# Key stacks by DMA, query projections by token halves, ordered VectorE norm chains and later low weight parts in a two-layer fp32 block

## The chip, the cores and the metric

The kernel runs on one core of a Trainium2 chip. The metric is the device time of one execution in microseconds (us). The engines are called as the profile calls them: PE (TensorE), PEld (its weight loads), DVE (VectorE), ACT (ScalarE), POOL (GpSimd) and SP (the engine that issues the DMAs).

## The reference

Two transformer layers on 512 latent tokens and 256 context tokens, width 1024, in fp32. Layer 0 mixes with gated linear recurrences, layer 1 with windowed attention (16 query heads of 64, 4 key heads, context keys, a sink). Each layer is followed by a gated feed-forward part, and each branch goes through a root-mean-square norm and a residual sum. Only the latent tokens are returned.

```python
for l in range(DEPTH):                       # DEPTH = 2
    u_lat = modulate(x_lat, ng[0], ml[0], ml[1])
    u_ctx = modulate(x_ctx, ng[0], mc[0], mc[1])
    if l % 2 == 0:
        y_lat, y_ctx = recurrent_mixer(...)
    else:
        y_lat, y_ctx = attention_mixer(...)  # q, k, v = u @ w_qkv, rope, softmax, @ w_o
    x_lat = x_lat + ml[2] * rms_norm(y_lat, ng[1])
    h_lat = swiglu(modulate(x_lat, ng[2], ml[3], ml[4]), ffn_w_in[l], ffn_w_out[l])
    x_lat = x_lat + ml[5] * rms_norm(h_lat, ng[3])
    ...                                      # the same for the context, in layer 0
```

## The kernel before

Activations lie transposed: 128 partitions hold 128 of the 1024 channels, the free axis holds tokens, and eight such tiles make a stream. For fp32 accuracy each product is made of three: weights and activations are split into a high part (`hi`, rounded) and a low part (`lo`, the rest), and PE adds hi·hi, hi·lo and lo·hi. `wload` fetches a weight tile of 128x1024 by a DMA on SP (`raw`, 4 buffers), makes `whi` on ACT or POOL and `wlo` on DVE or POOL (3 buffers each). Which engine does which is set for each phase by `engines(ph)`: a list for the high parts (a = ACT, p = POOL) and one for the low parts (d = DVE, p = POOL), taken in turn. `whold` does the same and keeps the parts (`kwh`, `kwl`). One accumulation over 1024 channels is 24 matmuls.

Work is written as Python generators, one step per yield. `drain` runs one to its end, and `merge(main, side, ratio)` puts `ratio` steps of `side` behind each step of `main`. The framework then schedules by a timeline of its own, so the order on each engine is a planner's, except where `follow(key, ins)` chains an instruction behind the last one of the same key and engine.

Two passages between stages matter here. At the first, layer 0's feed-forward output `po` ends in two token halves `HS[0]`, `HS[1]`; `lat_next(h)` then does the residual sum and the next norm of half h (`residual`: `y` times the norm factor, added into `xl`; `Acc.add`: squares on ACT, summed on POOL or DVE into `acc`; `rstd_bc`: a sum over partitions on PE, root, reciprocal, broadcast on PE into `ps_tr`; `norm_mod`: `nt`, `uh` on ACT, `ul` on DVE). The K and V projections of context and latent halves (`kv_ctx`, `kv_lat`) run beside `lat_next(1)`. Then come the first four Q projections (`q_lat(range(4))`, 512 tokens wide) and the attention scores, and the other four Q projections beside these. `k_stack` writes each 64-row key head twice, into both halves of the partitions, high and low parts apart (`KC`, `KL`): four ACT copies and four DVE subtractions for each pair of heads.

At the second passage the attention output projection `wo(1)` runs beside `lat_next2(0)`, and layer 1's first feed-forward tiles (`ffn_in`, phase `f1`) beside `lat_next2(1)`.

Of the kernel before, what the change touches and what calls it, by code (L numbers as in the profile page):

```python
# [11 lines left out]
F32 = mybir.dt.float32  # L12
# [7 lines left out]
P = 128  # L20
# [25 lines left out]
def block_kernel(ctx, tc, plan, xT, cT, vecs, w2, cst, atm, rope, ada, rec_a, rec_v, rec_g, rec_o, qk_w, v_w, wo_w, ff_in, ff_out, out):  # L46
# [8 lines left out]
    def uid(s):  # L55
        state["n"] += 1
        return f"{s}{state['n']}"
# [56 lines left out]
        return tiles[k // st.r][:, k % st.r, :]  # L114


    cfg = {"hi": "p", "lo": "d", "n": 0, "pri": 0, "evp": 150, "ll": False}

    def wload(src, n):
        with ExitStack() as es:  # L120
            if cfg["pri"]:
                es.enter_context(tc.high_priority(offset=cfg["pri"]))
            raw = wp.tile([P, 1024], F32, name=uid("raw"), tag="raw", bufs=WB + 1)
            nc.sync.dma_start(out=raw[:, :n], in_=src)
            hi = wp.tile([P, 1024], F32R, name=uid("whi"), tag="whi", bufs=WB)
            lo = wp.tile([P, 1024], F32R, name=uid("wlo"), tag="wlo", bufs=WB)
            q = cfg["n"]
            cfg["n"] += 1
            if cfg["hi"][q % len(cfg["hi"])] == "p":
                nc.gpsimd.tensor_scalar(hi[:, :n], raw[:, :n], 1.0, 0.0, ALU.mult, ALU.add)  # L130
            else:
                nc.scalar.copy(hi[:, :n], raw[:, :n])  # L132
            (nc.gpsimd if cfg["lo"][q % len(cfg["lo"])] == "p" else nc.vector).tensor_sub(  # L133
                lo[:, :n], raw[:, :n], hi[:, :n].bitcast(F32))
        return hi, lo

    def whold(src, n=1024):
# [245 lines left out]
            a.add(t, full(st))  # L383
        return a

    def norm_mod(tiles, acc, G, sh, j, u, sl, st=None):
# [6 lines left out]
        key = uid("nm") if 1 else None  # L393

        def low(i, t):
            if acc is None and 0:
# [28 lines left out]
            low(*v_)  # L425
        yield

    def residual(tiles, ys, yacc, gg, j, xacc, sl, pat=""):

        st = yacc.st  # L430
        bc = rstd_bc(yacc, sl)
        key = uid("res") if 1 else None
        yield
        for i in range(st.ntile):
            y = ys[i][:, :, sl]
            p_ = pat and pat[i] == "p"
# [12 lines left out]
            if xacc is not None:
                xacc.add(tiles[i][:, :, sl], sl, None, i >= st.ntile - 0)  # L450
            yield

    def new_u(st, alloc=None):
# [79 lines left out]
    def engines(ph):  # L533
        cfg["pri"] = {}.get(ph, 200)
        cfg["ll"] = ph in []
        cfg["hi"], cfg["lo"] = {'co': ['a', 'ddp'], 'rb': ['p', 'ddp'], 'ci': ['a', 'd'], 'kv': ['a', 'ddp'], 'wo': ['pa', 'd'], 'l0': ['a', 'd'], 'f1': ['a', 'd'], 'lo2': ['p', 'dp'], 'kw': ['a', 'd']}.get(ph, ("p", "d"))

    def drain(*gens):
        for g in gens:
# [747 lines left out]
    u3 = new_u(SL)  # L1287

    def lat_next(h):
        yield from residual(xl, yl2, yla2, gg2, 0, xla, HS[h], {'ln1': 'pppppppp', 'lw1': 'dpdpdpdp', 'lw0': 'pdddpddd', 'la0': 'dpdpdpdd', 'la1': 'dpdpdpdd', 'ln0': 'dddpdddp', 'cm': 'pdddpddd', 'lm': 'dddpdddp'}.get("ln%d" % h, ""))  # L1290
# [61 lines left out]
    def kv_ctx():  # L1352
        for m in range(2):
            p_ = qk_proj(8 + m, uc3, SC, FC)
            kc = ut([P, 256], name="kc")
            nc.scalar.copy(kc, p_)
            k_stack(kc, m, 0, 256)
            yield
        yield from v_proj(SC, uc3, range(2), 0)

# [6 lines left out]

    QS = {}

    def q_lat(ms):  # L1370
        for m in ms:
            y = roped(qk_proj(m, u3, SL, FL), FL)
            for h in range(2):
                q = ut([P, 512], F32R, name="QS")
# [4 lines left out]
                QS[2 * m + h] = q  # L1379
# [357 lines left out]
```

## Time and profile before

| | |
|---|---|
| three runs, median (lowest to highest) | 1818.57 us (1816.07 to 1819.11) |
| the profiled execution, its own time | 1819.26 us |
| span of its profile | 1817.5 us |
| PE busy in the span | 1744.9 us, 96% |
| DVE, ACT, POOL busy | 1058.1, 741.9, 437.6 us |

The span is what the profiler saw between the first and the last instruction; the execution's own time is 1.8 us longer. PE's busy time counts a matmul from its start to its modelled end, so a matmul at half clock, or one with a gap shorter than its own tail, also reads as busy.

### The profile page before, as it was taken

The page shows a single profiled execution, that of the slowest core. Times are in us where ns is not written, and L with a number is a line of the kernel's source. Part 1 is how long each engine was busy: PE and PEld are TensorE (multiplying, and loading weights), DVE is VectorE, ACT ScalarE, POOL GpSimd, SP SyncE. Part 2 cuts the span into 40 slices and gives each one's busy share as a digit, 9 for nine tenths or more (in the row PEclk, how much of TensorE's full clock was granted, in tenths as well). Part 3 has the DMA queues.
Part 4 walks back from the last instruction along what each step waited for, and adds up shares of the span by engine and source line. Part 5 has one row for each costly group of instructions (what it writes and reads, how often), then busy time and mean ns, then how long its engine had stood idle before and what let it go on. Part 6 is the DMA issues. An engine that isn't in the chain of part 4 may idle for free. (4 is left out here: it accounts for less than half of the span.)

```text
span 1817.5 us, 27788 instructions
## 1 busy us (share of the span) xinstructions
PE 1744.9 (96%) x10991; PEld 1482.3 (82%) x10991; DVE 1058.1 (58%) x1717; ACT 741.9 (41%) x1309; POOL 437.6 (24%) x460
## 2 busy tenths in 40 slices
PE   6899999999899999999999999899899899999997
PEld 3887778788798999988888888787677898888886
DVE  4986444664856744898642535679855853322336
ACT  3653445342654644542222222444665652222211
POOL 3655412433411004500000002424444400000015
PEclk8989999999999999999999999889999999999999
DMA  9435557212143554576554423402011343233323
GB/s 337 127 96 176 173 170 250 88 50 68 47 140 117 168 175 134 164 270 220 166 180 135 152 73 101 130 25 71 12 48 47 116 126 97 90 94 109 101 65 113
DMA packets 83699, 228.15 MB, mean 126 GB/s; under 512 B 9297, under 2 KB 14161, under 8 KB 83569
## 3 DMA queue, kind: packets, MB, share of 16 engines
q1 hardware_dynamic: 83568, 226.38, 38.6%
q8 instruction: 86, 1.41, 0.3%
q14 instruction: 45, 0.36, 0.1%
HBM read 224.25 MB, written 2.10 MB: 125 GB/s over the span
## 5 line engine op out<-in xcount | busy, mean ns | idle before, releaser
L133 DVE TENSOR_TENSOR wlo<-raw,whi 128x1024 fp32r<-128x1024 f32 (+3 forms) x296 | 358.7, 1213 | 315.0 <-ACT whi L132 234.2
L132 ACT CAST whi<-raw 128x1024 fp32r<-128x1024 f32 (+2 forms) x199 | 201.1, 1012 | 466.7 <-issue 177.7
L130 POOL TENSOR_SCALAR whi<-raw 128x1024 fp32r<-128x1024 f32 (+1 forms) x113 | 126.2, 1119 | 774.2 <-PE ps_mm L180 354.4
L180 PE MATMUL ps_mm<-uh,whi 128*128 128x256 f32 (+1 forms) x840 | 290.9, 347 | 2.1 <-POOL whi L130 1.9
L180 PE MATMUL ps_mm<-uh,wlo 128*128 128x256 f32 (+1 forms) x840 | 287.1, 342 | 5.1 <-DVE wlo L133 5.1
L180 PE MATMUL ps_mm<-ul,whi 128*128 128x512 f32 (+1 forms) x840 | 287.4, 342 | 0.0
L180 PE MATMUL ps_kv<-uh,whi 128*128 128x512 f32 (+1 forms) x696 | 247.1, 355 | 0.0
L180 PE MATMUL ps_kv<-uh,wlo 128*128 128x512 f32 (+1 forms) x696 | 245.1, 352 | 1.6 <-DVE wlo L133 1.5
L180 PE MATMUL ps_kv<-ul,whi 128*128 128x512 f32 (+1 forms) x696 | 245.3, 352 | 0.0
L180 PEld LDWEIGHTS ps_mm<-uh,whi 128*128 128x128 f32 x840 | 161.6, 193 | 24.9 <-POOL whi L130 3.3
L180 PEld LDWEIGHTS ps_mm<-uh,wlo 128*128 128x128 f32 x840 | 161.4, 192 | 23.2 <-DVE wlo L133 5.8
L180 PEld LDWEIGHTS ps_mm<-ul,whi 128*128 128x128 f32 x840 | 161.6, 192 | 17.0 <-issue 0.5
L346 POOL TENSOR_TENSOR acc<-acc,sq 128x256 f32<-128x256 f32 (+1 forms) x79 | 91.5, 1160 | 257.1 <-ACT sq L345 256.4
L180 PEld LDWEIGHTS ps_kv<-uh,whi 128*128 128x128 f32 x696 | 132.1, 190 | 22.4 <-issue 2.5
L180 PEld LDWEIGHTS ps_kv<-uh,wlo 128*128 128x128 f32 x696 | 131.7, 189 | 19.5 <-DVE wlo L133 1.9
L180 PEld LDWEIGHTS ps_kv<-ul,whi 128*128 128x128 f32 x696 | 131.9, 190 | 17.3 <-issue 0.3
L191 PE MATMUL ps_mm<-wlo,uh 128*128 128x256 f32 x344 | 100.1, 292 | 8.7 <-DVE wlo L133 8.7
L190 PE MATMUL ps_mm<-whi,uh 128*128 128x256 f32 x344 | 102.1, 299 | 0.8 <-ACT gate L786 0.5
L283 DVE SCALAR_TENSOR_TENSOR aacc<-ar,s,aacc 128x512 f32<-128x512 f32 x112 | 81.7, 756 | 35.1 <-DMA ar<-in_ada_dram 34.3
L180 PE MATMUL ps_kv<-hh,whi 128*128 128x512 f32 (+1 forms) x282 | 100.2, 355 | 0.0
L180 PE MATMUL ps_kv<-hh,wlo 128*128 128x512 f32 (+1 forms) x282 | 100.0, 355 | 0.0
L180 PE MATMUL ps_kv<-hl,whi 128*128 128x512 f32 (+1 forms) x282 | 99.9, 354 | 0.0
(322 smaller groups left out, 3534.3 us busy)
## 6 DMA issues: line engine op xcount, KB each, us to landing
raw<-in_ff_in_dram SPq DMA_DIRECT2D x138, 512.0 KB, 3.6
ar<-in_ada_dram SPq DMA_DIRECT2D x192, 256.0 KB, 4.2
raw<-in_ff_out_dram SPq DMA_DIRECT2D x52, 512.0 KB, 3.5
raw<-in_rec_a_dram SPq DMA_DIRECT2D x34, 512.0 KB, 4.2
raw<-in_rec_v_dram SPq DMA_DIRECT2D x16, 512.0 KB, 3.6
raw<-in_rec_g_dram SPq DMA_DIRECT2D x16, 512.0 KB, 3.5
raw<-in_rec_o_dram SPq DMA_DIRECT2D x16, 512.0 KB, 4.3
raw<-in_wo_w_dram SPq DMA_DIRECT2D x14, 512.0 KB, 3.5
```

The lines of the kernel that those rows point to most:

```text
L130: nc.gpsimd.tensor_scalar(hi[:, :n], raw[:, :n], 1.0, 0.0, ALU.mult, ALU.add)
L132: nc.scalar.copy(hi[:, :n], raw[:, :n])
L133: (nc.gpsimd if cfg["lo"][q % len(cfg["lo"])] == "p" else nc.vector).tensor_sub(lo[:, :n], raw[:, :n], hi[:, :n].bitcast(F32))
L180: mm(ps_, a, b, start=(i == 0), stop=(i == len(q) - 1))
L190: mm(ps, ah, hi[:, s], start=(k == 0), stop=False)
L191: mm(ps, ah, lo[:, s], start=False, stop=False)
L283: nc.vector.scalar_tensor_tensor(a, raw, s_, a, ALU.mult, ALU.add)
L346: (nc.vector if i else nc.gpsimd).tensor_add(d, d, q)
```

## The change

1. `k_stack` makes the high and the low part of a pair of key heads once, 128 partitions wide (one ACT cast, one DVE subtraction), and writes both into both halves of `KC` and `KL` by eight DMAs on SP (64 partitions of 1 KB each). There are six such calls.
2. `q_lat` takes a token slice. The first four Q projections are done for `HS[0]` right behind `kv_lat(0)`, inside the merge with `lat_next(1)`, and for `HS[1]` behind `kv_lat(1)`. Their weights are loaded and split twice.
3. In phase `kv` all low weight parts are made on POOL (before: two of three on DVE).
4. `residual` and `norm_mod` take a key. Both halves of `lat_next` share the key `next`, so that on each engine these steps stand in the order of the program. `lat_next2` has one key for each half.
5. `lat_next(1)` adds six of its eight residual tiles on DVE instead of none; the squares of the last two tiles of `lat_next` and `lat_next2`, and of the last output tile of a half-width feed-forward end, are no longer summed on POOL or DVE but read by PE directly (`own`).
6. `behind`: in phase `f1` the low weight parts of `wload` stand behind the last DVE step of `lat_next2(0)`.

```diff
+    def behind(ins):
+        k = (cfg["behind"], str(ins.ins.engine))
+        if k in lane:
+            tc.add_manual_dep(ins.ins, lane[k], mybir.DependencyInfo(mybir.DependencyClass.NoSync,
+                                                                     mybir.DependencyReason.DATA), reason="behind")
...
-            (nc.gpsimd if cfg["lo"][q % len(cfg["lo"])] == "p" else nc.vector).tensor_sub(
-                lo[:, :n], raw[:, :n], hi[:, :n].bitcast(F32))
+            behind((nc.gpsimd if cfg["lo"][q % len(cfg["lo"])] == "p" else nc.vector).tensor_sub(
+                lo[:, :n], raw[:, :n], hi[:, :n].bitcast(F32)))
...
-                xacc.add(tiles[i][:, :, sl], sl, None, i >= st.ntile - 0)
+                xacc.add(tiles[i][:, :, sl], sl, None, i >= st.ntile - own)
...
-                    yacc.add(y, sl, 0, m >= KD - 0)
+                    yacc.add(y, sl, 0, n == 256 and m >= KD - 1)
...
     def lat_next(h):
-        yield from residual(xl, yl2, yla2, gg2, 0, xla, HS[h], {...}.get("ln%d" % h, ""))
-        yield from norm_mod(xl, xla, G1, ada1[0], 0, u3, HS[h])
+        yield from residual(xl, yl2, yla2, gg2, 0, xla, HS[h], "dddpdddp", "next", 2)
+        yield from norm_mod(xl, xla, G1, ada1[0], 0, u3, HS[h], key="next")
...
     def k_stack(src, m, c0, n):
-        for h in range(2):
-            kv = 2 * m + h
-            a = src[64 * h : 64 * h + 64, :n]
-            own, oth = slice(64 * h, 64 * h + 64), slice(64 - 64 * h, 128 - 64 * h)
-            kh, kl = kcols(0, kv, c0, n), kcols(1, kv, c0, n)
-            nc.scalar.copy(kh[own], a)
-            nc.scalar.copy(kh[oth], a)
-            nc.vector.tensor_sub(kl[own], a, kh[own].bitcast(F32))
-            nc.vector.tensor_sub(kl[oth], a, kh[own].bitcast(F32))
+        th, tl = ut([P, 512], F32R, name="kth")[:, :n], ut([P, 512], F32R, name="ktl")[:, :n]
+        nc.scalar.copy(th, src)
+        nc.vector.tensor_sub(tl, src, th.bitcast(F32))
+        for i, t in enumerate((th, tl)):
+            for h in range(2):
+                for o in range(2):
+                    nc.sync.dma_start(out=kcols(i, 2 * m + h, c0, n)[64 * o : 64 * o + 64].bitcast(F32),
+                                      in_=t[64 * h : 64 * h + 64].bitcast(F32))
...
     engines("kv")
-    drain(merge(seq(kv_ctx(), kv_lat(0)) if 1 else seq(kv_lat(0), kv_ctx()), lat_next(1), 2.5))
-    drain(kv_lat(1))
-    drain(q_lat(range(4)))
+    QH = range(4)
+    drain(merge(seq(kv_ctx(), kv_lat(0), q_lat(QH, HS[0])), lat_next(1), 2.5))
+    drain(kv_lat(1), q_lat(QH, HS[1]))
...
     engines("f1")
+    cfg["behind"] = "next2a"
```

Three places show how instructions move. In the rows, a name is the tile written, then those read; the last part is the shape.

The first is DVE at the first passage, inside the norm of latent half 0 (`nt`, `ul` with `ps_tr_11068` before, `ps_tr_11070` after). Before:

```order
L440 SCALAR_TENSOR_TENSOR y_8072<-y_8072,gv_3263,ps_tr_11164 128x256
L440 SCALAR_TENSOR_TENSOR y_8073<-y_8073,gv_3263,ps_tr_11164 128x256
L440 SCALAR_TENSOR_TENSOR y_8074<-y_8074,gv_3263,ps_tr_11164 128x256
L1326 TENSOR_TENSOR KC_11109<-kc_11147,KC_11107 64x256
L1327 TENSOR_TENSOR KC_11109<-kc_11147,KC_11107 64x256
L440 SCALAR_TENSOR_TENSOR y_8075<-y_8075,gv_3263,ps_tr_11164 128x256
L440 SCALAR_TENSOR_TENSOR y_8076<-y_8076,gv_3263,ps_tr_11164 128x256
L1326 TENSOR_TENSOR KC_11109<-kc_11147,KC_11107 64x256
L1327 TENSOR_TENSOR KC_11109<-kc_11147,KC_11107 64x256
L440 SCALAR_TENSOR_TENSOR y_8077<-y_8077,gv_3263,ps_tr_11164 128x256
L440 SCALAR_TENSOR_TENSOR y_8078<-y_8078,gv_3263,ps_tr_11164 128x256
L401 SCALAR_TENSOR_TENSOR ul_10929<-nt_11078,ada_8211,uh_10921 128x256
```

After:

```order
L408 SCALAR_TENSOR_TENSOR ul_10928<-nt_11080,ada_8211,uh_10920 128x256
L417 SCALAR_TENSOR_TENSOR nt_11088<-xl_7298,gv_10465,ps_tr_11070 128x256
L408 SCALAR_TENSOR_TENSOR ul_10929<-nt_11084,ada_8211,uh_10921 128x256
L417 SCALAR_TENSOR_TENSOR nt_11092<-xl_7300,gv_10465,ps_tr_11070 128x256
L408 SCALAR_TENSOR_TENSOR ul_10930<-nt_11088,ada_8211,uh_10922 128x256
L417 SCALAR_TENSOR_TENSOR nt_11096<-xl_7302,gv_10465,ps_tr_11070 128x256
L408 SCALAR_TENSOR_TENSOR ul_10931<-nt_11092,ada_8211,uh_10923 128x256
L417 SCALAR_TENSOR_TENSOR nt_11100<-xl_7304,gv_10465,ps_tr_11070 128x256
L408 SCALAR_TENSOR_TENSOR ul_10932<-nt_11096,ada_8211,uh_10924 128x256
L408 SCALAR_TENSOR_TENSOR ul_10933<-nt_11100,ada_8211,uh_10925 128x256
L451 TENSOR_TENSOR y_8071<-y_8071,ps_tr_11170 128x256
L454 SCALAR_TENSOR_TENSOR xl_7290<-y_8071,gv_3263,xl_7290 128x256
```

Before, the eight residual products of half 1 (L440) and the key subtractions (L1326, L1327) stand between the second and the third `ul` of half 0; after, all eight `ul` of half 0 stand ahead of the first residual step of half 1.

The second is PE behind the V projection of half 0 (`ps_kv_11433` before, `ps_kv_11451` after). Before:

```order
L191 MATMUL ps_kv_11433<-kwl_10916,uh_10926 128x256
L192 MATMUL ps_kv_11433<-kwh_10915,ul_10934 128x256
L369 MATMUL ps_tr_11299<-ident,rs_11297 128x128 x2
L180 MATMUL ps_kv_11464<-uh_10919,kwh_10837 128x256
L180 MATMUL ps_kv_11503<-uh_10919,kwh_10891 128x256
L190 MATMUL ps_mm_11542<-kwh_10901,uh_10919 128x256
```

After:

```order
L198 MATMUL ps_kv_11451<-kwl_10915,uh_10925 128x256
L199 MATMUL ps_kv_11451<-kwh_10914,ul_10933 128x256
L187 MATMUL ps_kv_11488<-uh_10918,whi_11484 128x256
L187 MATMUL ps_kv_11488<-ul_10926,whi_11484 128x256
L187 MATMUL ps_kv_11488<-uh_10918,wlo_11485 128x256
L187 MATMUL ps_kv_11488<-uh_10919,whi_11484 128x256
```

Before, the broadcast of half 1's norm factor (L369) and matmuls that need half 1's `uh` follow at once; after, four Q projections of half 0 (96 matmuls) stand between, with the sums of half 1's squares among them.

The third is ACT at the second passage, around the first `uh` of `lat_next2(0)` (`uh_13949` before, `uh_14137` after). Before:

```order
L132 CAST whi_14375<-raw_14373 128x1024
L459 COPY y_12722<-ps_mm_14066 128x256
L345 ACTIVATE sq_14098<-ps_mm_14066 128x256
L132 CAST whi_14426<-raw_14424 128x1024
L154 CAST kwh_14325<-raw_14323 128x512
L154 CAST kwh_14329<-raw_14323 128x512
L417 ACTIVATE uh_13949<-nt_14012,ada_9162 128x256
L417 ACTIVATE uh_13950<-nt_14015,ada_9162 128x256
```

After:

```order
L139 CAST whi_14566<-raw_14564 128x1024
L139 CAST whi_14620<-raw_14618 128x1024
L466 COPY y_12912<-ps_mm_14258 128x256
L352 ACTIVATE sq_14290<-ps_mm_14258 128x256
L424 ACTIVATE uh_14137<-nt_14204,ada_9162 128x256
L424 ACTIVATE uh_14138<-nt_14207,ada_9162 128x256
L161 CAST kwh_14472<-raw_14470 128x512
L161 CAST kwh_14476<-raw_14470 128x512
```

Two casts of kept parts have moved behind the first two `uh`; the two high parts of `f1` (`whi`) still stand ahead of them. On DVE the first low part of `f1` stood right ahead of the first `nt` before, and stands behind the last `ul` of that half after.

## Rows read from the trace of the kernel before

**Rows 1.** The page's first part: busy time, share of the span, instructions.

```profile
PE 1744.9 (96%) x10991; PEld 1482.3 (82%) x10991; DVE 1058.1 (58%) x1717; ACT 741.9 (41%) x1309; POOL 437.6 (24%) x460
```

**Rows 2.** Busy time by windows: length, PE, PEld, DVE, ACT, POOL, PEclk, DMA, GB/s.

```profile
1150.30:1218.60 68.30, 55.96 (x372) 53.50 (x371) 48.37 (x110) 29.89 (x73) 22.22 (x27) 0.83 0.16 49
1218.60:1234.70 16.10, 16.10 (x73) 13.33 (x72) 14.43 (x18) 3.30 (x5) 6.00 (x5) 1.00 0.21 67
1234.70:1320.00 85.30, 79.43 (x503) 59.52 (x502) 72.61 (x217) 50.74 (x119) 38.05 (x43) 1.00 0.12 38
...
1160.00:1167.00 7.00, 7.00 (x60) 7.00 (x60) 6.86 (x14) 2.40 (x6) 4.42 (x5) 1.00 0.47 145
```

**Rows 3.** PE's timeline at the first passage: start, length, tile, [idle before, releaser].

```profile
1153.12 0.80 PE L362 MATMUL ps_tr<-ones,acc 128*128 128x1 f32 x4 [2.57 <-POOL acc L346]
...
1176.23 0.42 PE L180 MATMUL ps_mm<-uh,kwh 128*128 128x256 f32 x1
...
1181.87 0.58 PE L180 MATMUL ps_kv<-ul,kwh 128*128 128x256 f32 x1 [5.22 <-DVE ul L401]
...
1198.59 0.80 PE L180 MATMUL ps_kv<-uh,kwh 128*128 128x256 f32 x2 [2.83 <-ACT uh L417]
...
1234.67 0.28 PE L1424 MATMUL ps_kv<-KC,QS 128*128 128x256 f32 x1
```

**Rows 4.** ACT's timeline there.

```profile
1151.37 0.42 ACT L345 ACTIVATE sq<-y 128x256 f32<-128x256 f32 x1 [1.33 <-DVE y L518]
```

**Rows 5.** DVE's timeline there.

```profile
1157.64 1.22 DVE L133 TENSOR_TENSOR wlo<-raw,whi 128x1024 fp32r<-128x1024 f32 x1
1158.78 0.41 DVE L444 TENSOR_TENSOR y<-y,ps_tr 128x256 f32<-128x256 f32 x1
1159.23 2.17 DVE L447 SCALAR_TENSOR_TENSOR xl<-y,gv,xl 128x256 f32<-128x256 f32 x1
...
1171.94 0.87 DVE L410 SCALAR_TENSOR_TENSOR nt<-xl,gv,ps_tr 128x256 f32<-128x256 f32 x2 [0.94 <-PE ps_tr L369]
```

**Rows 6.** POOL's timeline there.

```profile
1158.63 2.50 POOL L133 TENSOR_TENSOR wlo<-raw,whi 128x1024 fp32r<-128x1024 f32 x1 [4.88 <-ACT whi L132]
...
1175.20 4.73 POOL L442 TENSOR_TENSOR xl<-xl,y 128x256 f32<-128x256 f32 x6 [5.86 <-DVE y L440]
```

**Rows 7.** DVE's groups, forms apart, 1150 to 1235 us: count | busy, mean ns | idle before.

```profile
L401 DVE SCALAR_TENSOR_TENSOR ul<-nt,ada,uh 128x256 fp32r<-128x256 f32 x16 | 8.3, 516 | 0.8 <-ACT uh L417 0.7
...
L410 DVE SCALAR_TENSOR_TENSOR nt<-xl,gv,ps_tr 128x256 f32<-128x256 f32 x16 | 7.4, 474 | 1.0 <-PE ps_tr L369 0.9
...
L440 DVE SCALAR_TENSOR_TENSOR y<-y,gv,ps_tr 128x256 f32<-128x256 f32 x10 | 4.3, 475 | 0.0
...
L1326 DVE TENSOR_TENSOR KL<-ry,KL 64x256 fp32r<-64x256 f32 x8 | 3.4, 420 | 0.6 <-ACT KL L1324 0.2
...
L1327 DVE TENSOR_TENSOR KC<-kc,KC 64x256 fp32r<-64x256 f32 x4 | 2.5, 635 | 0.1
...
L444 DVE TENSOR_TENSOR y<-y,ps_tr 128x256 f32<-128x256 f32 x6 | 2.5, 410 | 0.0
```

**Rows 8.** The view of the tile `raw`, 1140 to 1235 us: its DMAs.

```profile
L124 SPq DMA_DIRECT2D raw<-in_qk_w_dram x8: 327/328/383, 1142.8 to 1221.9; - x8
DMA to landing us min/median/max: 3.5/3.6/4.4
```

**Rows 9.** The second passage, timelines of ACT, DVE and PE.

```profile
1430.07 1.05 ACT L132 CAST whi<-raw 128x1024 fp32r<-128x1024 f32 x1 [6.00 <-DMA raw<-in_ff_in_dram]
...
1431.15 1.22 DVE L133 TENSOR_TENSOR wlo<-raw,whi 128x1024 fp32r<-128x1024 f32 x1 [4.17 <-ACT whi L132]
...
1434.19 0.58 PE L180 MATMUL ps_mm<-uh,kwh 128*128 128x256 f32 x1 [3.52 <-ACT uh L417]
```

**Rows 10.** The end, timelines of POOL and DVE.

```profile
1805.35 0.72 POOL L346 TENSOR_TENSOR acc<-acc,sq 128x256 f32<-128x256 f32 x1 [0.67 <-ACT sq L345]
...
1806.72 0.50 DVE L447 SCALAR_TENSOR_TENSOR xl<-y,gv,xl 128x256 f32<-128x256 f32 x1
```

More of the change, by code (lines that the diff above doesn't have):

```diff
@@ L114, in ch @@
         return tiles[k // st.r][:, k % st.r, :]
-    cfg = {"hi": "p", "lo": "d", "n": 0, "pri": 0, "evp": 150, "ll": False}
+    cfg = {"hi": "p", "lo": "d", "n": 0, "pri": 0, "evp": 150, "ll": False, "behind": None}
+    def behind(ins):
[3 more added lines that the diff above has]
+                                                                     mybir.DependencyReason.DATA), reason="behind")
     def wload(src, n):
@@ L384, in sumsq, with norm_mod @@
         return a
-    def norm_mod(tiles, acc, G, sh, j, u, sl, st=None):
+    def norm_mod(tiles, acc, G, sh, j, u, sl, st=None, key=None):
         if acc is not None:
@@ L392, in norm_mod @@
         late = []
-        key = uid("nm") if 1 else None
+        key = key or uid("nm")
         def low(i, t):
@@ L426, in norm_mod, with residual @@
         yield
-    def residual(tiles, ys, yacc, gg, j, xacc, sl, pat=""):
+    def residual(tiles, ys, yacc, gg, j, xacc, sl, pat="", key=None, own=0):
         st = yacc.st
         bc = rstd_bc(yacc, sl)
-        key = uid("res") if 1 else None
+        key = key or uid("res")
         yield
@@ L535, in engines @@
         cfg["ll"] = ph in []
-        cfg["hi"], cfg["lo"] = {'co': ['a', 'ddp'], 'rb': ['p', 'ddp'], 'ci': ['a', 'd'], 'kv': ['a', 'ddp'], 'wo': ['pa', 'd'], 'l0': ['a', 'd'], 'f1': ['a', 'd'], 'lo2': ['p', 'dp'], 'kw': ['a', 'd']}.get(ph, ("p", "d"))
+        cfg["hi"], cfg["lo"] = {'co': ['a', 'ddp'], 'rb': ['p', 'ddp'], 'ci': ['a', 'd'], 'kv': ['a', 'p'], 'wo': ['pa', 'd'], 'l0': ['a', 'd'], 'f1': ['a', 'd'], 'lo2': ['p', 'dp'], 'kw': ['a', 'd']}.get(ph, ("p", "d"))
     def drain(*gens):
@@ L1289, in lat_next @@
     def lat_next(h):
-        yield from residual(xl, yl2, yla2, gg2, 0, xla, HS[h], {'ln1': 'pppppppp', 'lw1': 'dpdpdpdp', 'lw0': 'pdddpddd', 'la0': 'dpdpdpdd', 'la1': 'dpdpdpdd', 'ln0': 'dddpdddp', 'cm': 'pdddpddd', 'lm': 'dddpdddp'}.get("ln%d" % h, ""))
-        yield from norm_mod(xl, xla, G1, ada1[0], 0, u3, HS[h])
+        yield from residual(xl, yl2, yla2, gg2, 0, xla, HS[h], "dddpdddp", "next", 2)
+        yield from norm_mod(xl, xla, G1, ada1[0], 0, u3, HS[h], key="next")
     if "kv" == "po0":
@@ L1354, in kv_ctx @@
             p_ = qk_proj(8 + m, uc3, SC, FC)
-            kc = ut([P, 256], name="kc")
-            nc.scalar.copy(kc, p_)
-            k_stack(kc, m, 0, 256)
+            k_stack(p_, m, 0, 256)
             yield
@@ L1368, in block_kernel, with q_lat @@
     QS = {}
-    def q_lat(ms):
+    def q_lat(ms, sl=FL):
         for m in ms:
-            y = roped(qk_proj(m, u3, SL, FL), FL)
+            y = roped(qk_proj(m, u3, SL, sl), sl)
             for h in range(2):
-                q = ut([P, 512], F32R, name="QS")
+                if 2 * m + h not in QS:
+                    QS[2 * m + h] = ut([P, 512], F32R, name="QS")
+                q = QS[2 * m + h][:, sl]
                 a = y[64 * h : 64 * h + 64]
@@ L1378, in q_lat @@
                 nc.vector.scalar_tensor_tensor(q[oth], a, 0.125, q[own].bitcast(F32), ALU.mult, ALU.subtract)
-                QS[2 * m + h] = q
             yield
     engines("kv")
-    drain(merge(seq(kv_ctx(), kv_lat(0)) if 1 else seq(kv_lat(0), kv_ctx()), lat_next(1), 2.5))
-    adat[0] = "o"
-    if "kv" == "kv":
-        drain(ada_gen(1, tuple([]), ada1))
-    drain(kv_lat(1))
+    QH = range(4)
+    drain(merge(seq(kv_ctx(), kv_lat(0), q_lat(QH, HS[0])), lat_next(1), 2.5))
+    drain(kv_lat(1), q_lat(QH, HS[1]))
     H2.close()
@@ L1512, in lat_next2 @@
     def lat_next2(h):
-        yield from residual(xl, yw, ywa, gg1, 0, xla1, HS[h], {'ln1': 'pppppppp', 'lw1': 'dpdpdpdp', 'lw0': 'pdddpddd', 'la0': 'dpdpdpdd', 'la1': 'dpdpdpdd', 'ln0': 'dddpdddp', 'cm': 'pdddpddd', 'lm': 'dddpdddp'}.get("lw%d" % h, ""))
+        key = "next2" + "ab"[h]
+        yield from residual(xl, yw, ywa, gg1, 0, xla1, HS[h], ("pdddpddd", "dpdpdpdp")[h], key, 2)
         if not u4:
             u4.extend(new_u(SL))
-        yield from norm_mod(xl, xla1, G2, ada1[3], 0, u4, HS[h])
+        yield from norm_mod(xl, xla1, G2, ada1[3], 0, u4, HS[h], key=key)
     drain(merge(piped([(b, kv) for kv in range(4) for b in (2, 3)], AD), wo(0), 0.09))
@@ L1536, in block_kernel @@
                     ffn_in(SL, 1, u4, hl1, range(N0), HS[1], 0, hold_f, kf)), lat_next2(1), 2.2))
+    cfg["behind"] = None
     yf, yfa = new_ys(SL), Acc(SL, DY)
```

## The prediction

> **What bounds the kernel now.** I read the page's first part, then windows of the three places that the diff touches, then each engine's timeline there. PE is busy for 96% of the span [rows 1], so a gain must come from stretches in which PE waits or runs at half clock, or from fewer or cheaper matmuls. The change removes no product of the reference, so I looked for the lost time.
>
> The first passage reaches from 1150.3 us, where PE runs out of feed-forward work, to the first score at 1234.67 [rows 2, 3]: 84.4 us. The program has 312 matmuls of 256 columns and 96 of 512 in it. At full clock the first kind starts every 0.12 us (60 in 7.00 us) and the second every 0.22 us (73 in 16.10) [rows 2]: 37.4 and 21.6 us, 59 in sum. So some 25 us are lost. About 12.3 of them are open gaps (68.30 less 55.96 busy [rows 2]), mainly three. One is 2.57 us until POOL has summed the last squares. One is 5.22 us until DVE makes an `ul` of half 0. One is 2.83 us until ACT makes a `uh` of half 1 [rows 3]. The rest is half clock: the granted clock has a mean of 0.83 there and 1.00 in the windows behind [rows 2], and a single matmul's row reads 0.42 and 0.58 us there against 0.28 at full clock [rows 3].
>
> Why DVE is late is in its order and not in its load (48.4 of 68.3 us busy [rows 2]): eight residual products and four key subtractions stand between the `ul` tiles for which PE waits. POOL then needs 4.73 us for six of half 1's residual sums, and had waited 5.86 for DVE [rows 6].
>
> Elsewhere there is less to win. Scores take 79.4 us of PE in 85.3, with DVE at 72.6 [rows 2]. At the second passage PE waits 3.52 us for a `uh` [rows 9]. The end is a chain of POOL and DVE [rows 10].
>
> **The first passage, term by term.** I walk the chain in the new order, with durations from the rows.
>
> *Own squares.* Before, the last square ends on ACT at 1151.79 [rows 4] and PE reads the sum at 1153.12 [rows 3]. After, PE reads the square itself: it starts at about 1152.0, 1.1 us earlier. With the 24 matmuls that fill the broadcast (2.9 us) PE is at 1155.7 or so by then.
>
> *Residual of half 0.* It began at 1158.78, with a 1.22 us low part ahead of it on DVE [rows 5] that now is POOL's. I put the start at 1156.1. From there to the first `nt` it took 13.16 us (to 1171.94 [rows 5]). After, one POOL sum of 0.7 us less stands at its end (by the one at the end of the kernel [rows 10]), and more POOL low parts run beside it (below): I take 13.7, so `nt` at 1169.8. PE has 96 context matmuls (11.5 us) until 1167.3 and waits until the first `uh` at 1170.6: a gap of 3.3 us stays, in a new place.
>
> *Norm of half 0.* Its 16 steps now stand together. At 0.47 to 0.52 each by the means [rows 7], nearer 0.42 where nothing blocks, with two key low parts, they end at 1178. PE follows with 72 matmuls to about 1179.2. The 5.22 us gap is gone.
>
> *Residual of half 1.* On DVE behind that, with two rope sets (2 us) ahead of or between its tiles: 13.7 + 2, so `nt` at about 1194. Six tiles' sums are DVE's now, 6 x 0.50 [rows 10] against POOL's 4.73 [rows 6]. PE has one V and three Q accumulations of half 0 (96 matmuls, 11.5 us) until 1190.7, then waits for squares and a late POOL low part, and ends the fourth Q at about 1195. Here a wait of 2 to 3 us takes the place of the old 2.83.
>
> *Norm of half 1, then Q.* 16 norm steps and some 21 of rope and query rows at 0.43 (16 us), plus 5 us of blocking: 1215. PE runs 120 of its 192 matmuls within that and 72 behind (8.6 us): first score at 1223.6 against 1234.67. **Term 1: -11.2 us.** Splitting Q costs PE 192 x 0.12 against 96 x 0.22, about +1.5 us, and is in the walk. Bounds: if every new wait doubles, -5; if the gaps close and the clock stays at full, 60.5 us of matmuls (504 x 0.12) and some 6 of unavoidable chain remain, -18.
>
> **What blocks DVE.** A residual step with two operands from memory (L447) took 2.17 us at 1159.23 and ended at 1161.40, just behind a POOL low part that ran from 1158.63 to 1161.13 [rows 5, 6]. Alone it takes 0.50 [rows 10]. Steps with a PSUM operand (L444) keep 0.41 [rows 5, 7]. Context key subtractions take 635 ns where POOL sums beside them, against 420 for the same form on the latent keys [rows 7]. The change makes all eight low parts of Q on POOL, 2.50 us each [rows 6]: 20 us in which DVE could stand still. I take half of that, 10 us in all, of which some 7 are on the chain: DVE steps that read PSUM or that stand before PE's need go on, and the low parts whose weights come early lie under context work. Both ends: 0 and 16.
>
> The Trainium skill, page "SBUF — State Buffer", section "Who interferes with whom", has a rule that speaks against this change: a DVE instruction with two SBUF inputs contends with a GpSimd instruction that reads SBUF, and whichever issues first keeps the shared pair for its whole length. The row of 2.17 us agrees. By the rule alone each of the eight low parts would block a residual or norm step, and the gain would be the first rival's.
>
> **The key stacks.** DVE loses 24 subtractions at 0.42 to 0.64 [rows 7], about 11.5 us, and gains six of 128x256 (2.5) and the residual sums (3). The low parts that go to POOL free another 2.4 (2 x 1.22 [rows 5]); query rows in halves cost 1 to 2, blocking 10. DVE's load over both windows and the scores stays near 137 us: moved, not lowered. Less of it is left when the scores begin, where DVE is at 85%: **Term 2: -1.0 us** (0 to -3).
>
> The copies go to SP: 48 of 64 KB. No such transfer is in the trace; the nearest row is a 512 KB weight, 0.33 us to issue and 3.5 to 4.4 us to land [rows 8]. In the new order each copy waits for the one eight places earlier, so 48 go in six groups: 2.6 us each if issue alone counts (8 x 0.33), 4.4 if landing does. The first 32 stand behind the low parts of half 0's keys (about 1190) and end by 1198. Queued behind them is the fourth Q weight of half 1, needed near 1215: no cost. The last 16 follow at about 1217 and land by 1224 to 1226; the first score that reads these keys is near 1231. I cost them at nothing, hidden by the first scores; from 14 us for both groups on, each us would be paid.
>
> **The other terms.** *Second passage:* DVE's first `nt` there comes up to 4.17 us earlier, since no low part that waits for its weight stands ahead [rows 9]. But ACT still has two high parts ahead of the first `uh`, and the weight for them lands at 1430.07 [rows 9]; `uh` moves only by what is queued behind them. **Term 3: -2.5** (-1 to -5, between the low part's 1.22 and all that the low part holds up). *End:* 0.72 us of POOL goes [rows 10], but DVE's last residual step ends at 1807.2 and the factor behind the sum is needed after it. **Term 4: -0.4** (0 to -0.7). *Other stages:* the planner places instructions of layer 0's recurrences otherwise, without a change in the code. **Term 5: 0** (-3 to +3).
>
> Sum: -11.2 - 1.0 - 2.5 - 0.4 = -15.1, against this execution's 1819.26: 1804.2. It lies 0.7 above the median of 1818.57, so I predict 1803.5.
>
> **Rivals.**
> - *POOL's low parts block DVE fully (0.16).* For it: the 2.17 us row [rows 5]. Against: only steps that meet a low part wait. 16 us on the chain instead of 7 are 9 more, of which the Q matmuls that fill PE's waits cover 3: 6 us lost of term 1, 1809.5.
> - *DVE is the bound, so the order gains nothing (0.14).* For it: 72.6 of 85.3 us in the scores [rows 2], and a load that stays the same; what PE wins until the first score it gives back waiting for softmax steps. Term 1 shrinks to the 1.1 of the squares, with 0.4 of the end: 1817.
> - *Slower: the key copies (0.09).* SP's queue at half 1's last 16 copies, of 1 KB a row. If a group of eight takes 18 us and not 4.4, the scores wait from 1231 to 1253, 22 us against 15.1 won: +7, 1825. It decides from about 15 us a group on (1217 + 30 = 1247, 16 us lost). Against: 512 KB land in 4.4 [rows 8].
> - *Nothing blocks and the clock holds (0.13).* Term 1 is -18: 1796.5.
>
> **How the numbers follow.** The forecast has 0.48; its own range is 1798 to 1809. The range reaches from 1794 (the last rival with term 5 below nothing) to 1816, which leaves out the slower case and about half of the second rival. A measurement of this kernel can tell about 0.2%, 3.6 us, from no change. Faster by more: forecast, first and last rival, 0.77. Within it: the second, 0.14. Slower: 0.09.
>
> **What would show it.** In the changed profile the first score stands near 1224 in PE's timeline; the idle entries of 2.57 (POOL's sum) and 5.22 (`ul`) are gone, and one of about 3 us stands ahead of the first `uh` of half 0. Residual steps on DVE that overlap POOL's low parts read about 2 us. The mean granted clock of that window is above 0.86. The view of the key tiles shows landing times under 5 us and no PE wait on them. The prediction is wrong if the first score comes early but PE's idle time in the scores grows by as much (second rival), if PE waits for `KL` (third), or if stages ahead of 1150 us move by over 3 us.

## The result and the profile after

Six runs of the changed kernel have a median of 1831.55 us (1827.33 to 1834.70), six of the kernel before 1817.41 us: a ratio of 1.0082, 95% interval 1.0070 to 1.0094. It is 14 us slower, where I had forecast 15 us faster. The profiled execution took 1834.66 us, with a span of 1832.9.

The page's first part: PE is as busy a share as before [rows 1], of a longer span.

```profile
PE 1758.5 (96%) x11135; PEld 1493.7 (81%) x11135; DVE 1059.7 (58%) x1722; ACT 746.0 (41%) x1303; POOL 446.2 (24%) x457
```

Windows of the changed kernel, with the columns of [rows 2]: the first passage in two parts (from PE's last feed-forward matmul), then the same length of scores as in [rows 2].

```profile
1160.90:1220.50 59.60, 53.85 (x415) 53.46 (x414) 46.07 (x102) 27.24 (x58) 26.37 (x20) 0.91 0.37 106
1220.50:1235.48 14.98, 14.98 (x127) 14.98 (x126) 11.63 (x25) 3.04 (x7) 7.64 (x7) 1.00 0.34 89
1235.48:1320.80 85.32, 75.28 (x437) 53.65 (x436) 67.64 (x194) 44.40 (x105) 38.69 (x40) 0.96 0.17 54
```

PE's timeline at the passage:

```profile
1156.76 0.38 PE L369 MATMUL ps_tr<-ones,acc 128*128 128x1 f32 x2 [0.72 <-POOL acc L353]
...
1177.94 0.58 PE L187 MATMUL ps_kv<-uh,kwh 128*128 128x256 f32 x1 [0.65 <-ACT uh L424]
...
1211.33 0.47 PE L187 MATMUL ps_kv<-ul,kwh 128*128 128x256 f32 x1 [4.15 <-DVE ul L408]
...
1235.48 0.28 PE L1426 MATMUL ps_kv<-KC,QS 128*128 128x256 f32 x1
```

The passage did become shorter, and the old waits of 2.57 and 5.22 us [rows 3] have gone, but for 0.72 of the first. A new one of 4.15 us for an `ul`, now of half 1, has come. The scores do less in the same time (75.3 us of PE in 85.3 against 79.4 [rows 2]). I cut each profile at four places, by the start of the instruction: the first DMA of `ff_out` weights in layer 0 (SP's timeline) and, in PE's, the last feed-forward matmul ahead of the passage, the first score, the last product of softmax weights and values ("last PV"). Each stands behind the same projections in both kernels.

| us | `ff_out` | last ff. matmul | passage | scores to last PV | from there to the end |
|---|---|---|---|---|---|
| before | 671.2 | 1156.9 | 77.8 | 172.6 | 410.2 |
| after | 678.2 | 1160.9 | 74.6 | 186.0 | 411.4 |

By these two profiles 7 us are lost ahead of 680 us, where no edit lies (3 of them come back by 1161); 3 are won at the passage; 13 are lost in the scores. Two things are to be explained.

### The profile page after: what moved, and what is told of

Read it like the earlier page. It is cut to its first block, busy times and chain, and to the rows that moved or that the text cites. A ratio compares the mean times of both kernels' runs of the same rounds, so it can differ in the third digit from the quotient of the medians.

```text
span 1832.9 us, 28197 instructions
## 1 busy us (share of the span) xinstructions
PE 1758.5 (96%) x11135; PEld 1493.7 (81%) x11135; DVE 1059.7 (58%) x1722; ACT 746.0 (41%) x1303; POOL 446.2 (24%) x457
## 4 chain that ended last, share of the span: by engine, by line
PE 50%; DVE 6%; ACT 2%; issue 1%; DMA 1%; POOL 0%; SPq 0%; DVEq 0%; POOLq 0%; ACTq 0%
PE ps_kv L187 23%; PE ps_mm L187 20%; PE ps_o L1467 2%; PE ps_tr L1460 2%; DVE xl L454 1%; ACT P L1442 1%; DVE wlo L140 1%; DVE QS L1384 1%; PE ps_o L296 1%; PE ps_tr L369 1%; PE ps_kv L1426 1%; PE ps_kv L1427 1%; DMA raw<-in_ff_out_dram 1%; DVE ul L408 0%; DVE nt L417 0%
## 5 line engine op out<-in xcount | busy, mean ns | idle before, releaser
L187 PE MATMUL ps_mm<-uh,whi 128*128 128x512 f32 (+1 forms) x840 | 290.5, 346 | 1.8 <-POOL whi L137 1.8
L187 PE MATMUL ps_mm<-uh,wlo 128*128 128x512 f32 (+1 forms) x840 | 286.6, 342 | 5.1 <-DVE wlo L140 5.1
L187 PE MATMUL ps_kv<-uh,whi 128*128 128x512 f32 (+1 forms) x728 | 253.3, 348 | 0.0
L187 PE MATMUL ps_kv<-uh,wlo 128*128 128x512 f32 (+1 forms) x728 | 251.5, 346 | 1.6 <-DVE wlo L140 1.5
L187 PE MATMUL ps_kv<-ul,whi 128*128 128x512 f32 (+1 forms) x728 | 251.5, 345 | 0.0
L187 PEld LDWEIGHTS ps_kv<-uh,wlo 128*128 128x128 f32 x728 | 137.9, 189 | 18.7 <-DVE wlo L140 1.9
L187 PEld LDWEIGHTS ps_kv<-ul,whi 128*128 128x128 f32 x728 | 138.2, 190 | 16.1
L353 POOL TENSOR_TENSOR acc<-acc,sq 128x256 f32<-128x256 f32 (+1 forms) x71 | 84.0, 1184 | 253.2 <-ACT sq L352 252.6
L199 PE MATMUL ps_mm<-whi,ul 128*128 128x256 f32 x344 | 99.7, 291 | 0.0
L187 PE MATMUL ps_mm<-hh,wlo 128*128 128x256 f32 (+1 forms) x277 | 92.6, 334 | 2.8 <-DVE wlo L140 2.1
```

What stands on the lines that cost most here:

```text
L187: mm(ps_, a, b, start=(i == 0), stop=(i == len(q) - 1))
L199: mm(ps, al, hi[:, s], start=False, stop=(k == KD - 1))
L353: (nc.vector if i else nc.gpsimd).tensor_add(d, d, q)
```

## The experiments

**Which plan.** The program is laid out three times: `Plan` gives named tiles to slots by the order that the layout ahead of it came out with, and the program keeps the layout that its own estimate of the time puts first. The orders on the engines show that the kernel before kept its first and the changed kernel its second: up to 1145 us every kernel below with a first plan has the order of the kernel before on PE, DVE, ACT and POOL, instruction by instruction, and the changed kernel has that of `b_plan2`. So the comparison above changed two things at once. `a_plan1` is the changed kernel with its first plan, `b_plan2` the kernel before with its second, `l_plan2` and `l_plan3` a variant that stands below with its second and third.

```diff
-    for _ in range(3):
+    for _ in range(1):                     # 2 for the second plan
         nc, _, order, ns = program(Plan(uses, first, order))
-        if best is None or (ns < best[1] if "min" == "min" else True):
-            best = (nc, ns)
+        best = (nc, ns)
```

> The changed kernel, but with the first of the three plans of tile slots that its program makes (the kernel before runs with its first, the changed kernel with its second); up to the first passage its order on every engine is then that of the kernel before. Theory A (the 7 us that the changed kernel is behind by 650 us come from the second plan and not from an edit): the first feed-forward output of layer 0 is read at the same time as before within 1 us, the total is about 7 us under the changed kernel, 1.004 of before. Rival B (the edits themselves slow the earlier stages): still 7 us behind there, 1.008. Either way, the scores of the attention end some 8 us later after the feed-forward's end than before.

Measured: 1818.6 us, 1.0008 (0.9996 to 1.0021), 13 us under the changed kernel. Passage and scores together take 258.0 us against 250.4 before, the 8 us that were expected.

> The kernel before, with its second plan in place of its first; nothing else differs. Theory A: about 7 us slower than before, 1.004, all of it lost before 700 us, where its order is that of the changed kernel. Rival B: 1.000, no loss there.

Measured: 1828.1 us, 1.0057 (1.0040 to 1.0073). Theory A holds in its sign, and the second plan costs more than the 7 us: 10 us in the old code and 13 in the new. That all of it would be lost before 700 us does not hold (see below). Windows show the part ahead of the passage, with the columns of [rows 2]. First the kernel before, then the changed one, then `b_plan2`:

```profile
350.00:375.00 25.00, 25.00 (x160) 19.13 (x159) 12.76 (x19) 6.46 (x12) 7.77 (x6) 1.00 0.17 58
475.00:500.00 25.00, 23.09 (x172) 22.23 (x173) 19.82 (x26) 17.95 (x31) 5.16 (x4) 0.88 0.28 86
```

```profile
350.00:375.00 25.00, 24.87 (x139) 17.90 (x139) 12.78 (x20) 7.50 (x13) 7.82 (x6) 0.86 0.18 58
475.00:500.00 25.00, 18.24 (x126) 17.83 (x126) 23.60 (x30) 13.65 (x24) 7.86 (x11) 0.86 0.28 86
```

```profile
350.00:375.00 25.00, 25.00 (x142) 18.44 (x140) 12.05 (x18) 6.07 (x11) 7.82 (x6) 0.86 0.19 61
475.00:500.00 25.00, 19.57 (x142) 19.36 (x143) 22.50 (x29) 15.06 (x26) 7.56 (x10) 0.86 0.27 85
```

PE's timeline names the wait in the second window, in the changed kernel and in `b_plan2`:

```profile
493.86 0.35 PE L197 MATMUL ps_mm<-whi,uh 128*128 128x256 f32 x1 [3.06 <-ACT gate L793]
```

```profile
491.80 0.36 PE L190 MATMUL ps_mm<-whi,uh 128*128 128x256 f32 x1 [2.27 <-ACT gate L786]
```

In both kernels with the second plan the granted clock falls to 0.86 in the first window, and in the second PE is busy for 18 to 20 us and not 23. The kernel before has neither.

**Undoing one part, under the first plan.** `a_oldkeys` takes the old body of `k_stack`, `a_oldlows` the old engines of the low parts:

```diff
-'kv': ['a', 'p']
+'kv': ['a', 'ddp']
```

> The changed kernel with its first plan and the old key stacks (four ACT copies and four DVE subtractions a pair of heads, no DMA copies). Theory K (the copies over DMA, or the order that the planner gives the scores because of them, cost the time between passage and scores): 5 to 9 us less than the changed kernel with its first plan, near 0.999 of before. Rival D (DVE is the bound there, so that the 18 subtractions that come back cost more): 0 to 6 us more than it.

Measured: 1827.79 us, 1.0048 (1.0032 to 1.0065), 9 us over `a_plan1` by the medians and 7 by the ratios, with some 4 us of uncertainty: theory K falls, and the copies by DMA are worth rival D's 6 us or more.

> The changed kernel with its first plan, with the low weight parts of the phase of K, V and Q made by DVE, DVE, POOL in turn as before (all on POOL in the change). Theory P (POOL's low parts block DVE's norm and query steps at the first passage): 3 to 7 us less than the changed kernel with its first plan. Rival D (DVE is the bound): 2 to 5 us more. If neither engine is what PE waits for: within 1.5 us of it.

Measured: 1812.83 us, 0.9973 (0.9962 to 0.9984), 6 us under `a_plan1`: theory P.

`l_oldq` and `l_oldln` undo the Q halves or the fixed order of `lat_next` from there (the `q_lat` and the two `drain` lines of before; the `lat_next` of before).

> The changed kernel with its first plan, the low parts of K, V and Q made as before (as the run that stood at 0.9973 of before), and the first four Q projections 512 tokens wide behind all of K and V again. Theory Q (the halves fill PE's wait for half 1's norm): that wait comes back, 5 to 9 us, most of it at the window between half 0's V and half 1's first `uh`; 1.000 to 1.003. Rival S (what the halves win until the first score is given back in the scores, where DVE has the rows of three projections left): within 2 us of 0.9973.

Measured: 1817.22 us, 0.9995 (0.9985 to 1.0005); passage 77.1 us, scores 173.5.

> The same kernel (first plan, low parts as before, at 0.9973), with Q in halves and key copies by DMA, but with the residual and norm steps of the two latent halves unchained and their residual sums on POOL as before. Theory O (the fixed order takes away the wait of 5 us for an `ul` of half 0): 4 to 8 us slower, 1.000 to 1.002, and an idle entry of over 3 us ahead of a matmul of half 0 that waits for `ul`. Rival S: the first score comes later, but the scores are shorter; within 2 us of 0.9973.

Measured: 1817.55 us, 0.9997 (0.9987 to 1.0007); passage 71.5 us, scores 175.8. Both parts are worth some 4 us here, give or take 3: near the lower ends of theory Q and theory O, and not clearly outside the 2 us of the two rivals S. But theory O's mark is missing in `l_oldln`: no wait for an `ul` of half 0 comes back (the next runs say why), and what PE waits for instead is a `uh` of half 1, 2.39 us.

**Doing one part alone**, in the kernel before: the new `k_stack`, or the new `lat_next`.

> The kernel before with the new key stacks alone (DMA copies), its first plan. Theory K2 (the copies free DVE of 18 subtractions and ACT of 24 copies, some of which stand between `ul` tiles for which PE waits): 5 to 9 us faster, 0.995 to 0.997, and the wait of 5.22 us shrinks. Rival (they gain only together with the fixed order): within 2 us of before.

Measured: 1817.88 us, 0.9999 (0.9989 to 1.0009), and theory K2 falls in the total: by one profile the passage is 3 us shorter and the scores 2 us longer. PE's timeline has its mark, 0.83 us in place of 5.22 [rows 3]:

```profile
1174.93 0.58 PE L180 MATMUL ps_kv<-ul,kwh 128*128 128x256 f32 x1 [0.83 <-DVE ul L401]
```

> The kernel before with the fixed order of the two halves' residual and norm steps alone (key, six of eight residual tiles on DVE, own squares), its first plan. Theory O: the wait of 5.22 us goes, but PE has no Q work of half 0 to cover half 1's chain; 2 us slower to 3 us faster, 0.998 to 1.001. Rival (the order alone brings the gain that I forecast for the passage): 8 to 11 us faster, 0.994 to 0.996.

Measured: 1821.08 us, 1.0014 (1.0004 to 1.0024), at theory O's slow end and far from its rival. The wait for `ul` is gone here too, and a new one stands at half 1's sum of squares, which the order has put behind:

```profile
1191.54 0.59 PE L362 MATMUL ps_tr<-ones,acc 128*128 128x1 f32 x2 [4.08 <-DVE acc L346]
```

So the copies and the order each take the same wait away, and neither gains alone; with the halves of Q between, together, they do (`a_oldlows`; without the halves, `l_oldq`, they do not).

**More on plans and on the engine of a weight part**, from `a_oldlows`. `l_highs` adds `'at': ['a', 'd']` (high parts of the second four Q on ACT); `l_dve` has `'kv': ['a', 'd']`.

> The changed kernel with the low parts of K, V and Q made as before, with its second plan (with its first: 0.9973 of before). Theory A (the second plan is slower whatever the edits): 1.003 to 1.005, with PE at half clock near 350 us and a wait of 2 to 3 us for `gate` near 490 us, as in the changed kernel and in the kernel before with its second plan. Rival (plans and edits interact, the loss was one of the two kernels'): 0.997 to 0.999.

Measured: 1826.46 us, 1.0059 (1.0047 to 1.0072), 0.86 of the clock at 350 to 375 us and a wait of 3.05 us for `gate`. The third code, the same plan, the same marks.

> The same kernel with the third plan, the one that its program picks when it is left to choose. If the planner's own estimate picked well, 0.996 to 0.9975. Theory A2 (plans two and three share the order of the recurrences that costs the time): 1.000 to 1.004.

Measured: 1815.51 us, 1.0003 (0.9991 to 1.0015). The third plan has neither mark, yet is slower than the first by 3 us by the medians and 5 by the ratios, while the program's own estimate prefers it. So the number of theory A2 came, and its reason, a shared order of the recurrences, did not.

> The kernel at 0.9973 (first plan, low parts as before) with the high weight parts of the second four Q projections on ACT in place of POOL, where each took up to 2.0 us beside DVE's rows. Theory P2 (POOL work beside DVE slows DVE's query and score rows): scores 2 to 4 us shorter, 0.995 to 0.9965. Rival (ACT's softmax steps are then late): 0.998 to 1.000.

Measured: 1812.60 us, 0.9983 (0.9973 to 0.9993), with the scores at 173.8 us. Its median is that of `a_oldlows`; the scores are 1.8 us shorter in one profile, just under theory P2's 2 to 4, and the ratio is the rival's.

> The kernel at 0.9973 with all low parts of K, V and Q on DVE. Theory P (each low part on POOL costs DVE as long as it runs, 2.4 us against 1.2 on DVE itself): as fast or up to 2 us faster, 0.996 to 0.9975. Rival D (DVE's load counts): 2 to 5 us slower, 0.9985 to 1.000.

Measured: 1813.54 us, 0.9985 (0.9975 to 0.9995). The interval reaches into both ranges; it doesn't decide.

**Which low parts cost it, and the two small terms.** In `x_lows_half0` the line `cfg["lo"] = "ddp"` stands ahead of the second drain, in `x_lows_half1` `cfg["lo"] = "p"`, with the first drain at "ddp". `l_nobehind` leaves out `cfg["behind"] = "next2a"`, `l_noown` sets `own` to 0.

> The changed kernel with its first plan; the low parts of the Q weights for the first token half on POOL, those for the second half by DVE, DVE, POOL. (All on POOL: 1.0008; none changed: 0.9973.) Theory R (they cost by blocking DVE's residual steps): 0.9995 to 1.001, near the kernel with all on POOL. Rival N (the second half's cost it): within 1 us of 0.9973 to 0.998.

Measured: 1812.36 us, 0.9978 (0.9967 to 0.9988).

> The other way round: first half's low parts by DVE, DVE, POOL, second half's on POOL. Theory R: 0.997 to 0.998. Rival N (they block norm and query rows of the second half, so that DVE enters the scores late): 0.9995 to 1.001, with the scores 4 to 7 us longer than 175.6.

Measured: 1822.36 us, 1.0029 (1.0019 to 1.0039), scores 182.0 us. Rival N holds in its sign: the price comes with the second half's low parts. At 10 us over `a_oldlows` it is above the rival's range, and above the 6 us of `a_plan1`, which has both halves' on POOL: the two halves do not add up.

> The kernel at 0.9973 (first plan, low parts as before) without the rule that puts the low parts of the next feed-forward behind DVE's norm at the second passage. By the forecast's third term: 1 to 5 us slower, 0.998 to 1.000. Rival (`uh` waits for ACT and the weight's DMA anyway): within 1 us.

Measured: 1815.54 us, 0.9987 (0.9978 to 0.9996): 2.5 us by the ratios, as the forecast's term, but the intervals meet.

> The kernel at 0.9973 with all squares summed on POOL or DVE again and none read by PE itself. By the forecast (1.1 us at the first passage, 0.4 at the end): 1 to 2 us slower, 0.9978 to 0.9985. Rival (each of these sums stands on a chain that PE waits for, at three residuals): 3 to 6 us slower.

Measured: 1813.28 us, 0.9980 (0.9970 to 0.9991): 1 us, within what the runs can tell.

The stages of the main kernels, cut as above:

| us | last ff. matmul | passage | scores to last PV | to the end |
|---|---|---|---|---|
| before | 1156.9 | 77.8 | 172.6 | 410.2 |
| b_plan2 | 1158.9 | 74.9 | 179.2 | 413.4 |
| a_plan1 | 1152.7 | 75.8 | 182.2 | 408.9 |
| a_oldlows | 1155.6 | 69.4 | 175.6 | 409.0 |
| l_plan2 | 1160.4 | 75.8 | 176.2 | 410.4 |
| x_lows_half0 | 1153.4 | 69.4 | 176.1 | 413.0 |
| x_lows_half1 | 1157.1 | 71.8 | 182.0 | 411.7 |

Each is one profile; sums of a row differ from medians by some us. The fourteen kernels with a first plan have the same order up to 1145 us, and the last feed-forward matmul stands between 1152.0 and 1157.3 us in them. So a difference of up to 5 us in one column says little.

## Why the prediction was wrong

**Step one that failed: "Other stages: 0 (-3 to +3)".** I saw that the planner placed layer 0's recurrences otherwise and priced it at nothing. It was another plan of the whole program. By the ratios it costs 10, 13 and 16 us in three codes: the one before, the changed one, and the changed one with the old low parts (1.0057 against 1; 1.0082 against 1.0008; 1.0059 against 0.9973). That is nearly all of the measured loss, since the edits alone stand at 1.0008. My sign for it came: the stages ahead of 1150 us moved by over 3 us. At the recurrences the cost is seen as a half-clock stretch and a wait for `gate`, and 5 us of it lie ahead of the passage: the last feed-forward matmul stands at 1154.7 us in the mean of the fourteen profiles with a first plan, at 1160.1 in the three with a second. The rest has no fixed place. The scores are 7 us longer in `b_plan2` and 4 in the changed kernel than in the same code with the first plan, but in `l_plan2` they are not, and its passage is 6 us longer. Why the slots of the second plan make that order was not tried.

**Step two that failed: terms 1 and 2, the passage and the scores.** Without the plan the edits gain nothing. That is the second rival's time (1817, which I gave 0.14; `a_plan1` has 1818.6), by luck as far as its reason goes. Term 1 was -11.2, with bounds of -5 and -18: the passage is 3.2 us shorter in the changed kernel and 2.0 in `a_plan1`. Term 2 had the scores 1.0 us shorter: they are 9.6 longer in `a_plan1`. The rival's reason, that DVE is the bound and the order gains nothing, is only half of it: with the old engines for the low parts the order, the halves and the copies do gain 8.4 us at the passage, within my bounds, and lose 3.0 in the scores.

Some 5 us of the passage in `a_plan1` belong to that one execution. From the last feed-forward matmul on PE runs 369 matmuls in the same order as in `x_lows_half0`, and comes to the next one 4.9 us later. The windows, with the columns of [rows 2], show where, first in `x_lows_half0`, then in `a_plan1`. Behind the same 4.05 us of work in 5 us, the next 10 us run at full clock in one, and in the other at a mean of 0.56, so mostly at the lower of the clock's two levels (0.5).

```profile
1163.44:1168.44 5.00, 4.05 (x36) 3.97 (x34) 2.06 (x5) 1.38 (x4) 0.90 (x2) 1.00 0.00 0
1168.44:1178.44 10.00, 9.36 (x78) 9.21 (x78) 8.70 (x23) 5.53 (x14) 0.00 (x0) 1.00 0.33 94
```

```profile
1162.70:1167.70 5.00, 4.05 (x30) 3.97 (x29) 1.90 (x4) 1.15 (x4) 0.90 (x2) 0.85 0.00 0
1167.70:1177.70 10.00, 9.56 (x49) 9.47 (x50) 6.78 (x19) 5.33 (x14) 0.00 (x0) 0.56 0.25 75
```

**POOL's low parts: near in size, and the scores missed.** I put some 7 us of blocking on the chain, 5 of them on half 1's norm and query rows, and `a_oldlows` measures 6 in all. I read it off a residual step, the row of 2.17 us [rows 5]. Such steps are blocked again in the changed kernel, and so are query rows, on DVE and then on POOL:

```profile
1162.08 2.49 DVE L454 SCALAR_TENSOR_TENSOR xl<-y,gv,xl 128x256 f32<-128x256 f32 x1
1164.49 0.41 DVE L451 TENSOR_TENSOR y<-y,ps_tr 128x256 f32<-128x256 f32 x1
1164.94 2.18 DVE L454 SCALAR_TENSOR_TENSOR xl<-y,gv,xl 128x256 f32<-128x256 f32 x1
...
1205.73 4.69 DVE L1384 SCALAR_TENSOR_TENSOR QS<-ry,QS 64x256 fp32r<-64x256 f32 x2
1210.45 0.42 DVE L1342 TENSOR_TENSOR ry<-ry,rx 128x256 f32<-128x256 f32 x1
1210.79 0.48 DVE L408 SCALAR_TENSOR_TENSOR ul<-nt,ada,uh 128x256 fp32r<-128x256 f32 x1
```

```profile
1161.88 4.95 POOL L140 TENSOR_TENSOR wlo<-raw,whi 128x1024 fp32r<-128x1024 f32 x2 [1.32 <-ACT whi L139]
...
1205.16 2.40 POOL L140 TENSOR_TENSOR wlo<-raw,whi 128x1024 fp32r<-128x1024 f32 x1
1207.80 2.34 POOL L140 TENSOR_TENSOR wlo<-raw,whi 128x1024 fp32r<-128x1024 f32 x1 [0.24 <-ACT whi L139]
```

The two residual steps at 1162 and 1165 lose 4 us. In `x_lows_half0` they read 2.48 and 2.18 us too, and its total is within 1 us of `a_oldlows`: PE has context work there. The two query rows at 1205.73 take 4.69 us in place of 0.87, since two POOL low parts lie over them; behind them in DVE's order stands the `ul` for which PE then waits 4.15 us at 1211.33. With the first plan less of it is left: PE waits 1.76 us for such an `ul` in `x_lows_half1` and 1.04 in `a_oldlows`. The Trainium skill, page "SBUF — State Buffer", section "Who interferes with whom", says that a DVE instruction with two SBUF inputs contends with a GpSimd instruction that reads SBUF. The trace agrees with it in both places, and only the second stands ahead of a row that PE waits for.

DVE's groups from 1195 to 1245 us give the same, 2.6 us more for the query rows: first `a_oldlows`, then `x_lows_half1`, count | busy, mean ns.

```profile
L1384 DVE SCALAR_TENSOR_TENSOR QS<-ry,QS 64x256 fp32r<-64x256 f32 x16 | 7.2, 452 | 1.4 <-ACT QS L1383 1.0
```

```profile
L1384 DVE SCALAR_TENSOR_TENSOR QS<-ry,QS 64x256 fp32r<-64x256 f32 x16 | 9.8, 615 | 1.4 <-ACT QS L1383 0.9
```

The scores are longer too with the second half's low parts on POOL, by 6 us (182.0 against 175.6 and 176.1), and the walk had nothing for that. The whole of the scores, with the columns of [rows 2], first in `a_oldlows`, then in `x_lows_half1`:

```profile
1224.95:1400.53 175.58, 168.00 (x1158) 128.65 (x1157) 120.81 (x366) 100.68 (x248) 78.77 (x91) 0.99 0.16 50
```

```profile
1228.89:1410.94 182.05, 171.89 (x1158) 128.25 (x1157) 121.87 (x368) 101.55 (x248) 77.76 (x91) 0.97 0.15 48
```

PE is idle for 10.2 us in place of 7.6, and the mean clock is 0.97 in place of 0.99: by length times what the clock lacks, an estimate, 5.5 us against 1.8. Together that is about the 6 us. But the order differs as well: it is the same on PE, DVE, ACT and POOL in `a_oldlows` and `x_lows_half0`, and another in `x_lows_half1` from about PE's 28th matmul on. No run keeps the order and moves the parts, so whether the blocked rows or the other order costs the scores those 6 us stays open.

A single gap does not tell it either. Early in the scores PE waits for `mx`, in `a_plan1` and then in `a_oldlows` (columns: length, PE busy, PEclk, DMA, GB/s), for much the same time; only the half clock behind it is longer in the first:

```profile
1243.49:1248.49 5.00, 4.63 (x21) 1.00 0.34 105
1248.49:1253.49 5.00, 3.15 (x11) 0.81 0.33 105
1253.49:1258.49 5.00, 5.00 (x22) 0.51 0.27 78
```

```profile
1239.95:1244.95 5.00, 5.00 (x26) 1.00 0.31 105
1244.95:1249.95 5.00, 3.19 (x14) 0.82 0.29 105
1249.95:1254.95 5.00, 5.00 (x34) 0.84 0.36 105
```

**What held.** The wait of 5.22 us for half 0's `ul` went. A wait at half 0's first `uh` came, but of 0.65 us and not 3.3. The wait for POOL's sum reads 0.72 us in place of 2.57, yet 2.39 in `a_oldlows`, which has the own squares too: they are worth the 1 us of `l_noown` at most. The mean clock of the passage rose above 0.86 (0.91 and 1.00). The second passage: PE waits 2.07 us there and not 3.52 [rows 9], and `l_nobehind` gives 2.5 us for the term of 2.5, within its uncertainty. At the end the row that answers to [rows 10] shows the sum gone, and a square in its place on which PE waits 1.81 us, so term 4 is too small to be seen.

```profile
1447.06 0.58 PE L187 MATMUL ps_mm<-uh,kwh 128*128 128x256 f32 x1 [2.07 <-ACT uh L424]
...
1820.85 0.38 PE L369 MATMUL ps_tr<-ones,sq 128*128 128x1 f32 x2 [1.81 <-ACT sq L334]
```

The third rival did not come. The key tiles' views (first `kth`, then SP's timeline) have a landing time of 2.0 us a copy, and no score waits for a DMA:

```profile
L1332 SPq DMA_DIRECT2D KC<-kth x8: 467/595/1096, 1180.4 to 1188.1; - x8
...
DMA to landing us min/median/max: 1.9/2.0/3.6
```

```profile
1235.03 2.46 SPq L1332 DMA_DIRECT2D KL<-ktl  x4
```

Four copies take SP 2.46 us, so a group of eight takes 5 and not the 2.6 to 4.4 that I had, and the last land near 1239.5 us: 4 us behind the first score, as priced, at nothing. What the copies buy beside the other edits, 7 to 9 us by `a_oldkeys`, I had only as a freed load on DVE and put at 1.0; alone, in `b_newkeys`, they buy nothing.

## What to carry to other kernels

Where a program picks one of several layouts by its own estimate, an edit is measured together with a draw of the layout: hold the layout, and run the old code with the new one too, before a word is said about the edit. Work that an off-path engine does beside a busy one is priced where it meets the rows that somebody waits for, not by how much it blocks in all: the same parts cost nothing on one token half, and moving the other half's cost over 5 us, though part of that may be the other order that the planner then gave the scores. The version to keep is the change with its first plan and the old engines for the low parts: 0.9973 (0.9962 to 0.9984) of the kernel before.

## What the runs showed that I had not expected

A copy of 64 KB between two places of SBUF takes SP about 0.60 us to issue and lands after 2.0 us, against 0.33 us to issue for a weight of 512 KB [rows 8]: 48 of them hold SP's queue for nearly 30 us. A half-clock stretch can come in one execution and not in another whose order is the same: behind the same 4.05 us of work in 5 us, 10 us at a mean of 0.56 in `a_plan1` and at 1.00 in `x_lows_half0`, which is 5 us at the passage. That is as much as most of the effects looked for, so stages of single profiles carry them only where many runs of the whole agree.
